# Two of the four weight sums of a block chunk made by accumulating transfers, and 23 block chunks in place of 20

## The chip, the cores and the metric

The kernel runs on one core of one Trainium2 chip. The metric is the device time of one execution in microseconds (us), lower is better. Engines are named as the profile names them: PE is TensorE's matmuls and PEld its weight loads, DVE is VectorE, ACT is ScalarE, POOL is GpSimd and SP is SyncE; the last two issue transfers (DMAs) here. PSUM is the memory that TensorE writes to, in eight banks of 512 fp32 values per partition.

## The reference

One layer over 512 tokens of 1024 channels, with 256 context tokens that give further keys and values. One combined projection yields ten parts of 1024 columns; half of them feed a gated convolution, the others a neighbourhood attention and the gates that merge both.

```python
h = _rmsnorm(x, pre_g[i]) * (1.0 + sc[:, None, :]) + sh[:, None, :]
...
parts = _split_in(h @ w_in[i])           # b, c, x, z_a | q, k, v, z_b | g_a, g_b
q = _apply_rope(_heads(parts[4]), cos, sin)
k = _apply_rope(_heads(parts[5]), cos, sin)
...
attn = _neighbourhood_attention(q, k, v, k_c, v_c, rpb[i])
y_a = (jax.nn.silu(z_a) * b_gate * _dwconv3(c_gate * x_in, conv_w, conv_b)) @ w_out_conv
y_b = (jax.nn.silu(z_b) * attn_o) @ w_out_attn
merged = jax.nn.sigmoid(g_a) * y_a + jax.nn.sigmoid(g_b) * y_b
x = x + gt[:, None, :] * _rmsnorm(merged @ w_o, post_g[i])
```

## The kernel before

**Products.** Every fp32 operand is split into a high part (a ScalarE cast to a type that TensorE multiplies at full speed, L67) and a low part (a VectorE subtraction, L68). A product is three matmuls: high by high, high by low, low by high.

**Chunks.** The weights of the projections come as 45 chunks of 1024 rows by 256 columns, that is two units of 128 output channels. Each is loaded as two `raw` tiles of 512 KB, for the upper and the lower 512 rows (`Chunk`, L87; three buffers of `raw`, four of the split weights `w`). They are named by what they yield: `cx` and `bz` for the convolution (two of its parts each), `qk` (a query and a key unit), `v`, `zb` (the attention's gate), `g0` to `g7` (the merge gates), `y0` to `y7` (both out projections). The last stage, after the y chunks, is the out projection with `w_o`.

- A plain chunk takes 2 x 8 x 3 = 48 matmuls of 512 columns.
- A block chunk halves rows, tokens and units, so that the weights are four blocks: B11 and B12 (columns 0 to 127 and 128 to 255 of the upper raw tile; `b11`, `b12` in the code), B21 and B22 (of the lower one). Seven block products in place of eight are made of four blocks or sums on the weights' side and as many on the tokens' side: T1 = B11 + B12, T2 = T1 + B22, T3 = B12 + B22, T4 = B21 + T2. Each of the seven is 12 matmuls of 256 columns, 84 in all (`product`, L287). The sums of the tokens are made once (`block_sums`), those of the weights for every chunk, in place in the raw tiles, on VectorE: L100 (T1), L103 (T2), L107 (T3), L108 (T4).

`pair` (L291) is the block chunk's program. It multiplies B11, B21, T1 and T2 in its first half, copies two banks into SBUF as snapshots on the way (L298, L301, L303, on ScalarE), then T4, T3 and B22 in its second half, with a copy (L309) and VectorE's combining operations (L312, L315). It uses three banks `a`, `b`, `e`. `Chunk.first` prepares what the first half needs and runs one chunk ahead; `Chunk.second` splits T3, T4 and B22 when the pair begins. A `qk` chunk is the exception: its B12 is kept for the context keys, so T3's sum is made in `second`. The chunk after it is loaded by `chunk.more()` in the middle of the pair. `paired` (L231) says which chunks are blocks: all g, qk3, qk4 and qk6, zb0 to zb2, cx and bz from 5, 20 in all.

**Stages.** At the start, conditioning and norms beside the first conv chunks, in an order written by hand. Then the attention: 64 steps of (pair of heads p, head, 128 queries), eight to each p, with the chunks of `plan` (L217) spread over the steps of their p; scores, softmax, transposes and the gather of values stand between them. `later` holds back queries and keys by some steps, until their rope is done. Behind the last step comes zb3, then g2 and g3, beside which the slices of the conv result `u` and of the attention are split into `us0` to `us7` and `as0` to `as7`; then y0, g4, y1, g5, ... in the order of `merge` (L236).

**Order.** Apart from the start, a scheduler places the instructions on each engine; the program's text gives their priority. Each engine then runs its own list in that order, and an instruction that waits holds up what stands behind it. SP's queue carries the weight loads. GpSimd's queue carries rope's accumulating transfers (L624, `tc<-tb`) and the copies of queries and keys between partitions, some 104 transfers in all.

Of the kernel before, what the change touches and what calls it, by code (L numbers as in the profile page):

```python
# [12 lines left out]
ALU = mybir.AluOpType  # L13
AX = mybir.AxisListType

P = 128
D = 1024
KT = 8
S = 512
# [8 lines left out]
def layer(ctx: ExitStack, tc, xp, ctxt, ctxT, cc, wmod, small, wfirst, win, wout, wo, rel, tab, out):  # L28
    nc = tc.nc
# [33 lines left out]

    def split(H, L, src, scale=None):

        if scale is None:
            nc.scalar.copy(H, src)  # L67
            nc.vector.tensor_sub(L, src, H.bitcast(F32))  # L68
        else:
            nc.scalar.mul(H, src, scale)  # L70
            nc.vector.scalar_tensor_tensor(
                out=L, in0=src, scalar=scale, in1=H.bitcast(F32), op0=ALU.mult, op1=ALU.subtract
            )
# [7 lines left out]
    class Chunk:  # L81
# [14 lines left out]
        def first(self, keep=False):  # L96
            (b11, b12), (b21, b22) = self.b = [(r[:, :, :P], r[:, :, P:]) for r in self.raws]
            t, sums = (wtile([P, 2, 2, 4, P]) for _ in range(2))
            split(t[:, 0, 0], t[:, 0, 1], b11)
            nc.vector.tensor_add(b11, b11, b12)  # L100
            split(sums[:, 0, 0], sums[:, 0, 1], b11)
            split(t[:, 1, 0], t[:, 1, 1], b21)
            nc.vector.tensor_add(b11, b11, b22)  # L103
            split(sums[:, 1, 0], sums[:, 1, 1], b11)
            self.keep = keep
            if not keep:
                nc.vector.tensor_add(b12, b12, b22)  # L107
            nc.vector.tensor_add(b21, b21, b11)  # L108
            self.B = {"B11": t[:, 0], "B21": t[:, 1], "T1": sums[:, 0], "T2": sums[:, 1]}
            return self  # L110

        def second(self):
            t, last = (wtile([P, 2, 2, 4, P]) for _ in range(2))
            (_, b12), (b21, b22) = self.b
            if self.keep:
                split(last[:, 1, 0], last[:, 1, 1], b12)
                nc.vector.tensor_add(b12, b12, b22)
            for n, x, b in (("T3", t[:, 0], b12), ("T4", t[:, 1], b21), ("B22", last[:, 0], b22)):
                split(x[:, 0], x[:, 1], b)
                self.B[n] = x  # L120
            self.B["B12"] = last[:, 1]

# [108 lines left out]
    def paired(n, i):  # L231
        return n == "g" or n == "qk" and i in (3, 4, 6) or n == "zb" and i < 3 or n in ("cx", "bz") and i > 4

# [48 lines left out]
    blocks_h = {}  # L282
# [8 lines left out]

    def pair(c1, c2, w=None):

        w = w or chunk().B
        a, b, e = (pj()[:, :256] for _ in range(3))
# [7 lines left out]
        nc.scalar.copy(c2[:, first], a)  # L303
        nc.vector.tensor_add(c1[:, first], c1[:, first], b)
        chunk.more()
        yield
        product(b, A22, w["T4"], True)
        product(a, blocks_h["S3"], w["T3"], False)
        nc.scalar.copy(c1[:, second], a)  # L309
        product(e, blocks_h["S4"], w["B22"], False)  # L310
        for cols, x in ((second, c1[:, second]), (first, e)):
            nc.vector.scalar_tensor_tensor(  # L312
                out=c2[:, cols], in0=c2[:, cols], scalar=-1.0, in1=x, op0=ALU.mult, op1=ALU.subtract
            )
        nc.vector.tensor_add(c1[:, second], c1[:, second], b)  # L315

# [339 lines left out]
    def keys_queries(p):  # L656
# [3 lines left out]
        if blocks:  # L660
            for _ in pair(q, k, w.B):
                yield
# [19 lines left out]

        def keys(src, cols):
            split(ks[0][:, cols], lows[:, cols], src)

        def rest():
            keys(k, slice(0, S))
            nc.gpsimd.dma_start(ks[1][lo], ks[0][hi])
# [513 lines left out]
```

## Time and profile before

| | |
|---|---|
| median of 3 runs | 709.33 us (709.26 to 709.7) |
| the profiled execution | 710.12 us |
| its span, first to last instruction | 708.3 us |
| granted TensorE clock, mean | 0.999 |
| DVE, second busiest engine | 585.2 us, 83% |
| ACT | 437.2 us, 62% |
| block products (L287) on PE | 216 us in 1680 matmuls |
| T3 and T4 sums (L107, L108) on DVE | 25.3 us in 37 additions |

The profile is of one execution. Its page gives the busy time of each engine, the chain of work that ended last (followed back from the last instruction to what released each step), and the costliest groups of instructions: the line, the engine, the operation with its output and input by the program's names, how many, the busy time and the mean, the idle time before them and what ended it. The trace can be asked for the same in any stretch, for what one tile waits for, and for the instructions in order of time.

### The profile page before, as it was taken

How to read it: one execution, taken by the hardware profiler on the slowest of the kernel's cores; microseconds unless marked ns; L12 is line 12 of the kernel's file. 1: busy time of each engine (PE TensorE's matmuls, PEld its weight loads, DVE VectorE, ACT ScalarE, POOL GpSimd, SP SyncE). 2: the span in 40 equal slices, each digit the busy share in tenths (PEclk: the TensorE clock that was granted, in tenths of full speed). 3: DMA queues.
4: the chain of work that ended last, by engine and by line, in shares of the span. 5: the costliest groups of instructions: out<-in, count | busy, mean ns of one | idle time of the engine just before them, and what ended most of it. 6: DMA issues, size and time to landing. Idle time of an engine off the chain costs nothing.

```text
span 708.3 us, 11424 instructions
## 1 busy us (share of the span) xinstructions
PE 695.4 (98%) x4196; PEld 618.5 (87%) x4196; DVE 585.2 (83%) x1114; ACT 437.2 (62%) x868; POOL 66.9 (9%) x110
## 2 busy tenths in 40 slices
PE   7999999999999999999999999999999999999996
PEld 4888888888889989898999999999898899988885
DVE  6979997668599989978898797999799675665996
ACT  6566632656577678765886676888694444442563
POOL 0000002240130310401302103000000000000000
PEclk9999999999999999999999999999999999999999
DMA  8996896565341563642636436313733233570013
GB/s 341 407 348 228 281 339 172 134 163 143 100 99 29 137 157 119 151 125 61 168 106 171 94 127 154 104 60 98 250 115 120 88 119 120 186 261 30 31 59 120
DMA packets 37466, 108.27 MB, mean 153 GB/s; under 512 B 5025, under 2 KB 5281, under 8 KB 37410
## 3 DMA queue, kind: packets, MB, share of 16 engines
q1 hardware_dynamic: 28946, 92.20, 38.0%
q0 software_dynamic: 8320, 15.21, 10.7%
q8 instruction: 33, 0.54, 0.3%
q14 instruction: 23, 0.19, 0.1%
q10 hardware_dynamic: 144, 0.13, 0.1%
HBM read 87.07 MB, written 5.24 MB: 130 GB/s over the span
## 4 chain that ended last, share of the span: by engine, by line
PE 88%; DVE 5%; DMA 3%; ACT 2%; issue 1%; SPq 0%; POOL 0%; DVEq 0%; ACTq 0%
PE ps L287 23%; PE ps L162 11%; PE ps L163 11%; PE ps L164 11%; PE ps L175 6%; PE ps L1006 5%; PE ps L771 4%; PE ps L180 3%; PE ps L752 3%; PE ps L715 3%; PE ps L194 2%; PE ps L422 2%; PE ps L426 2%; PE ps L423 2%; DMA fraw<-in_wfirst 1%; DVE w L68 1%
## 5 line engine op out<-in xcount | busy, mean ns | idle before, releaser
L67 ACT CAST w<-raw 128x512 fp32r<-128x512 f32 (+1 forms) x193 | 137.2, 731 | 91.4 <-PE ps L164 30.7
L68 DVE TENSOR_TENSOR w<-raw,w 128x512 fp32r<-128x512 f32 (+1 forms) x193 | 156.3, 824 | 41.8 <-ACT w L67 41.0
L287 PE MATMUL ps<-S,w 128*128 128x256 f32 x960 | 122.0, 283 | 1.2 <-ACT tc L303 1.2
L287 PEld LDWEIGHTS ps<-S,w 128*128 128x128 f32 x960 | 118.1, 192 | 1.5 <-ACT tc L303 1.4
L287 PE MATMUL ps<-h,w 128*128 128x256 f32 x720 | 94.2, 284 | 0.5 <-DVE tc L315 0.4
L287 PEld LDWEIGHTS ps<-h,w 128*128 128x128 f32 x720 | 89.9, 191 | 2.5 <-DVE tc L315 0.9
L162 PE MATMUL ps<-h,w 128*128 128x512 f32 x208 | 81.5, 392 | 0.0
L164 PE MATMUL ps<-h,w 128*128 128x512 f32 x208 | 81.2, 390 | 0.0
L163 PE MATMUL ps<-h,w 128*128 128x512 f32 x208 | 81.0, 390 | 0.0
L624 POOL DMA_DIRECT2D tc<-tb x32 | 28.8, 1175 | 301.9 <-DVE tc L622 182.6
L164 PEld LDWEIGHTS ps<-h,w 128*128 128x128 f32 x208 | 39.0, 188 | 8.2
L67 ACT CAST TH<-ps 128x512 fp32r<-128x512 f32 x64 | 36.0, 588 | 16.5 <-PE ps L752 16.4
L162 PEld LDWEIGHTS ps<-h,w 128*128 128x128 f32 x208 | 39.1, 188 | 8.0
L163 PEld LDWEIGHTS ps<-h,w 128*128 128x128 f32 x208 | 39.1, 188 | 7.9
L731 DVE CUSTOM_DVE_ANT_1 ps<-ps,bt 128x512 f32<-128x512 f32 x56 | 38.8, 694 | 8.4 <-PE ps L715 8.2
L745 ACT ACTIVATE pt<-pt,z 128x512 f32<-128x512 f32 x64 | 42.9, 721 | 4.6 <-DVE z L743 4.3
L68 DVE TENSOR_TENSOR TL<-ps,TH 128x512 fp32r<-128x512 f32 x64 | 42.4, 681 | 0.8 <-ACT TH L67 0.7
L752 PE MATMUL ps<-ident,pt 128*128 128x128 f32 x256 | 33.2, 273 | 0.0
L175 PE MATMUL ps<-w,h 128*128 128x512 f32 x128 | 32.3, 394 | 0.0
L752 PEld LDWEIGHTS ps<-ident,pt 128*128 128x128 f32 x256 | 29.3, 140 | 2.1
L738 ACT ACTIVATE pt<-ps,m 128x512 f32<-128x512 f32 x32 | 22.0, 689 | 10.8 <-DVE m L731 10.0
L771 PE MATMUL ps<-TH,V 128*128 128x256 f32 (+1 forms) x96 | 28.4, 318 | 0.0
(249 smaller groups left out, 1387.6 us busy)
## 6 DMA issues: line engine op xcount, KB each, us to landing
raw<-in_win SPq DMA_DIRECT2D x74, 512.0 KB, 4.5
wm<-in_wmod SPq DMA_DIRECT2D x34, 512.0 KB, 6.4
raw<-in_wout SPq DMA_DIRECT2D x16, 512.0 KB, 3.8
bt<-in_rel SPq DMA_DIRECT2D x16, 256.0 KB, 3.0
tc<-tb POOLq DMA_DIRECT2D x32, 128.0 KB, 3.8
B<-in_wo SPq DMA_DIRECT2D x8, 512.0 KB, 7.4
fraw<-in_wfirst SPq DMA_DIRECT2D x8, 384.0 KB, 8.7
qd<-qd POOLq DMA_DIRECT2D x24, 128.0 KB, 2.4
```

Source lines behind the costliest of these rows:

```text
L67: nc.scalar.copy(H, src)
L68: nc.vector.tensor_sub(L, src, H.bitcast(F32))
L162: nc.tensor.matmul(ps, lhsT=H[k][:, cs], rhs=mH[k], start=k == 0, stop=False)
L163: nc.tensor.matmul(ps, lhsT=H[k][:, cs], rhs=mL[k], start=False, stop=False)
L164: nc.tensor.matmul(ps, lhsT=L[k][:, cs], rhs=mH[k], start=False, stop=k == KT - 1)
L175: nc.tensor.matmul(ps, lhsT=mH[k][:, ts], rhs=both[k].rearrange("p a c -> p (a c)"), start=k == 0, stop=False, skip_group_check=True,)
L287: nc.tensor.matmul(ps, lhsT=w[:, x, k], rhs=act[y][k], start=start and k + o == 0, stop=k == 3 and o == 2, skip_group_check=True,)
L731: nc.vector.tensor_tensor_reduce(out=s3, in0=s3, in1=bt[:, e::4 - e][:, 0:2], scale=-1.0, scalar=3.0e38, op0=ALU.add, op1=ALU.min, accum_o ...
L745: nc.scalar.mul(x, x, z[:, i:i + 1])
L752: nc.tensor.transpose(tp[:, c], pt[:, c * P:(c + 1) * P], ident)
L771: nc.tensor.matmul(o3[:, dst], lhsT=V[p][:, kt, h], rhs=src(t), start=n == 0 and t is TH, stop=n == len(work) - 1 and t is TL,)
L1006: nc.tensor.matmul(out, lhsT=a(x, k, ts), rhs=w[y][k // 2][:, k % 2, cols], start=start and k + o == 0, stop=k == 3 and o == 2, skip_group ...
```

## The change

**Transfers for two sums.** T3 and T4 are no longer added on VectorE. `nc.gpsimd.dma_start(b12, b22, accum_op=ALU.add)` adds B22 to B12 inside SBUF, and the same adds T2 to B21. The first is issued behind T1's sum, the second behind T2's sum, both on GpSimd's queue, 256 KB each. T3 of a `qk` chunk stays on VectorE, since its B12 is needed. So that a block is one run of values in each partition, the host lays out the block chunks' weights by blocks.

**Later casts.** `second` splits B22 alone (and B12 of a `qk` chunk). The splits of T3 and T4 go to a new `third`, called behind the first half's snapshots, and their casts are pinned there with `tc.keep_in_program_order`: the scheduler can't move them ahead of the snapshots or behind what follows in the text. In the second half the products are now B22, T3, T4 in place of T4, T3, B22.

**More blocks.** qk5, qk7 and zb3 become block chunks, 23 in all.

**Keys.** The cast of a block chunk's keys (in `rest`) is pinned in the text's order too.

```diff
--- before.py
+++ after.py
@@ -61,10 +61,12 @@
     usc = [dr.tile([P, S], F32, name=f"usc{j}") for j in range(KT)]
     asc = [dr.tile([P, 2, S], F32, name=f"asc{g}") for g in range(2)]
 
-    def split(H, L, src, scale=None):
+    def split(H, L, src, scale=None, pinned=False):
 
         if scale is None:
-            nc.scalar.copy(H, src)
+            cast = nc.scalar.copy(H, src)
+            if pinned:
+                tc.keep_in_program_order(cast)
             nc.vector.tensor_sub(L, src, H.bitcast(F32))
         else:
             nc.scalar.mul(H, src, scale)
@@ -94,31 +96,38 @@
             return tuple([t[i // 4][:, i % 4, y] for i in k] for y in range(2)) + ([t[i // 4][:, i % 4] for i in k],)
 
         def first(self, keep=False):
-            (b11, b12), (b21, b22) = self.b = [(r[:, :, :P], r[:, :, P:]) for r in self.raws]
+            (b11, b12), (b21, b22) = self.b = [
+                [x[:, 2 * u:2 * u + 2].rearrange("p k (x c) -> p (k x) c", c=P) for u in range(2)] for x in self.raws
+            ]
             t, sums = (wtile([P, 2, 2, 4, P]) for _ in range(2))
             split(t[:, 0, 0], t[:, 0, 1], b11)
             nc.vector.tensor_add(b11, b11, b12)
+            if not keep:
+                nc.gpsimd.dma_start(b12, b22, accum_op=ALU.add)
             split(sums[:, 0, 0], sums[:, 0, 1], b11)
             split(t[:, 1, 0], t[:, 1, 1], b21)
             nc.vector.tensor_add(b11, b11, b22)
+            nc.gpsimd.dma_start(b21, b11, accum_op=ALU.add)
             split(sums[:, 1, 0], sums[:, 1, 1], b11)
             self.keep = keep
-            if not keep:
-                nc.vector.tensor_add(b12, b12, b22)
-            nc.vector.tensor_add(b21, b21, b11)
             self.B = {"B11": t[:, 0], "B21": t[:, 1], "T1": sums[:, 0], "T2": sums[:, 1]}
             return self
 
         def second(self):
-            t, last = (wtile([P, 2, 2, 4, P]) for _ in range(2))
-            (_, b12), (b21, b22) = self.b
+            last = wtile([P, 2, 2, 4, P])
+            (_, b12), (_, b22) = self.b
             if self.keep:
                 split(last[:, 1, 0], last[:, 1, 1], b12)
                 nc.vector.tensor_add(b12, b12, b22)
-            for n, x, b in (("T3", t[:, 0], b12), ("T4", t[:, 1], b21), ("B22", last[:, 0], b22)):
-                split(x[:, 0], x[:, 1], b)
+            split(last[:, 0, 0], last[:, 0, 1], b22)
+            self.B["B22"], self.B["B12"] = last[:, 0], last[:, 1]
+
+        def third(self):
+            t = wtile([P, 2, 2, 4, P])
+            (_, b12), (b21, _) = self.b
+            for n, x, b in (("T3", t[:, 0], b12), ("T4", t[:, 1], b21)):
+                split(x[:, 0], x[:, 1], b, pinned=True)
                 self.B[n] = x
-            self.B["B12"] = last[:, 1]
 
 
     behind = None
@@ -229,7 +238,7 @@
         "cx": lambda j: win[2 * j], "bz": lambda j: win[2 * j + 1],
     }
     def paired(n, i):
-        return n == "g" or n == "qk" and i in (3, 4, 6) or n == "zb" and i < 3 or n in ("cx", "bz") and i > 4
+        return n == "g" or n == "qk" and i > 2 or n == "zb" or n in ("cx", "bz") and i > 4
 
     order = [(win[i], False) for i in range(8)] + [(qk(0), False), (vz(0, 0), False)]
     order += [(where[n](i), n if paired(n, i) else False) for f in plan for n, i in f] + [(vz(3, 1), paired("zb", 3))]
@@ -289,9 +298,10 @@
                     skip_group_check=True,
                 )
 
-    def pair(c1, c2, w=None):
-
-        w = w or chunk().B
+    def pair(c1, c2, c=None):
+
+        c = c or chunk()
+        w = c.B
         a, b, e = (pj()[:, :256] for _ in range(3))
         first, second = slice(0, 256), slice(256, S)
         product(a, A11, w["B11"], True)
@@ -302,16 +312,17 @@
         product(a, blocks_h["S2"], w["T2"], False)
         nc.scalar.copy(c2[:, first], a)
         nc.vector.tensor_add(c1[:, first], c1[:, first], b)
+        c.third()
         chunk.more()
         yield
-        product(b, A22, w["T4"], True)
+        product(e, blocks_h["S4"], w["B22"], False)
         product(a, blocks_h["S3"], w["T3"], False)
         nc.scalar.copy(c1[:, second], a)
-        product(e, blocks_h["S4"], w["B22"], False)
-        for cols, x in ((second, c1[:, second]), (first, e)):
+        for cols, x in ((first, e), (second, c1[:, second])):
             nc.vector.scalar_tensor_tensor(
                 out=c2[:, cols], in0=c2[:, cols], scalar=-1.0, in1=x, op0=ALU.mult, op1=ALU.subtract
             )
+        product(b, A22, w["T4"], True)
         nc.vector.tensor_add(c1[:, second], c1[:, second], b)
 
     def both_units():
@@ -658,7 +669,7 @@
         q, k = both_units()
         blocks = paired("qk", p)
         if blocks:
-            for _ in pair(q, k, w.B):
+            for _ in pair(q, k, w):
                 yield
             rope(q, q)
             rope(k, k)
@@ -680,11 +691,11 @@
                     nc.gpsimd.dma_start(t[1][o], t[0][hi])
                 nc.gpsimd.dma_start(t[0][hi], t[0][lo])
 
-        def keys(src, cols):
-            split(ks[0][:, cols], lows[:, cols], src)
+        def keys(src, cols, pinned=False):
+            split(ks[0][:, cols], lows[:, cols], src, pinned=pinned)
 
         def rest():
-            keys(k, slice(0, S))
+            keys(k, slice(0, S), blocks)
             nc.gpsimd.dma_start(ks[1][lo], ks[0][hi])
             nc.gpsimd.dma_start(ks[1][hi], lows[hi])
             nc.gpsimd.dma_start(ks[0][hi], lows[lo])
@@ -1143,6 +1154,9 @@
     ui = units(a["w_in"][0]).copy()
     ui[q:v] = ui[q:v][..., channels]
     win = chunks(ui, order)
+
+    for n in [*range(10, 16), *(16 + 4 * (p // 2) + p % 2 for p in range(3, 8)), *range(19, 32, 4), *range(32, 40)]:
+        win[n] = win[n].reshape(128, 2, 4, 2, 128).transpose(0, 1, 3, 2, 4).reshape(128, 8, 256)
     uo = np.concatenate([units(a["w_out_conv"][0]), units(a["w_out_attn"][0])])
 
     wfirst = np.ascontiguousarray(win[:3].transpose(2, 1, 0, 3)).reshape(8, 128, 768)
```

The scheduler's lists move in the tail. The next rows are ScalarE's list around g2 and g3 before: `raw_5753` and `raw_5754` are g2's two raw tiles, `raw_5938` is g3's first, `us` are the slices of `u`, `ur` their sources, and L782 is zb3's tanh.

```order
L67 CAST w_5875<-raw_5753 128x512
L67 CAST w_5875<-raw_5754 128x512
L67 CAST us1_5959<-ur1_5851 128x512
L67 CAST us2_5962<-ur2_5852 128x512
L67 CAST us3_5965<-ur3_5853 128x512
L782 ACTIVATE tb_5842<-ps_5817 128x512
L67 CAST w_5876<-raw_5754 128x512
L67 CAST us4_6009<-ur4_5854 128x512
L298 COPY g2_5874<-ps_5883 128x256
L67 CAST us5_6012<-ur5_5855 128x512
L67 CAST us6_6015<-ur6_5856 128x512
L67 CAST w_5942<-raw_5938 128x512
```

After the change the list has these rows from the third snapshot of g2 on (L313); `raw_5952` and `raw_5953` are g2's tiles, `raw_6127` is g3's first, and `as` are the slices of the attention.

```order
L313 COPY g2_6063<-ps_6067 128x256
L67 CAST w_6122<-raw_5952 128x512
L67 CAST w_6122<-raw_5953 128x512
L67 CAST us7_6207<-ur7_6046 128x512
L67 CAST as0_6284<-ta_6047 128x512
L67 CAST as1_6287<-tb_6048 128x512
L67 CAST as2_6290<-ta_6049 128x512
L320 COPY g2_6063<-ps_6067 128x256
L67 CAST as3_6293<-tb_6050 128x512
L67 CAST w_6131<-raw_6127 128x512
L67 CAST as4_6337<-at4_3893 128x512
L67 CAST as5_6340<-at4_3893 128x512
```

g2's casts of T3 and T4 (`w_6122`) stood ahead of the pair's first snapshot and stand behind its third now; g3's first cast (B11) stood behind us6 and stands behind us7 and as0 to as3.

ScalarE's list in zb3 after the change, where zb3 is a block chunk: `raw_5788` and `raw_5789` are its tiles, `tc` its two units, and `raw_5952` and `w_5956`, `w_5957` belong to g2.

```order
L308 COPY tc_5887<-ps_5892 128x256
L67 CAST w_5819<-raw_5788 128x512
L311 COPY tc_5888<-ps_5894 128x256
L313 COPY tc_5888<-ps_5892 128x256
L67 CAST w_5947<-raw_5788 128x512
L67 CAST w_5947<-raw_5789 128x512
L67 CAST w_5956<-raw_5952 128x512
L787 COPY ta_5983<-ps_5970 64x512
L67 CAST us0_6145<-ur0_6039 128x512
```

Two new casts, T3 from `raw_5788` and T4 from `raw_5789`, stand between zb3's last snapshot and g2's B11; before, zb3 was plain and its casts were done ahead of its matmuls.

TensorE's list in y3 changes at the fourth slice of `u`: `w_6862` and `w_6863` are y3's two halves, `ps_6927` is the unit fed by `u` and `ps_6953` the one fed by the attention.

```order
L171 MATMUL ps_6927<-us4_6198,w_6863 128x512
L172 MATMUL ps_6927<-us4_6198,w_6863 128x512
L171 MATMUL ps_6953<-as0_6284,w_6862 128x512
L172 MATMUL ps_6953<-as0_6284,w_6862 128x512
L173 MATMUL ps_6953<-as0_6284,w_6862 128x512
L173 MATMUL ps_6927<-us4_6198,w_6863 128x512
```

Before, the three of us4 stood together; now the matmul with the low part of y3's second half (L173) has three of the other unit ahead of it.

## The prediction

> **What bounds the kernel now.** I read the page's head first, then the chain, then the busy time by stretches.
>
> ```profile
> span 708.3 us, 11424 instructions
> ...
> PE 695.4 (98%) x4196; PEld 618.5 (87%) x4196; DVE 585.2 (83%) x1114; ACT 437.2 (62%) x868; POOL 66.9 (9%) x110
> ...
> PE 88%; DVE 5%; DMA 3%; ACT 2%; issue 1%; SPq 0%; POOL 0%; DVEq 0%; ACTq 0%
> ```
>
> TensorE is busy for 98% of the span and the chain is 88% TensorE: VectorE's sums, which the change takes away, are not what ends last. So the change can gain in two ways only: fewer matmul microseconds, and fewer waits of TensorE. It loses wherever TensorE must wait for a weight block that comes later than now. The stretches show how much room there is.
>
> ```profile
> core 0: us, PE busy (x) PEld busy (x) DVE busy (x) ACT busy (x) POOL busy (x), PEclk, DMA share, GB/s
> ...
> 321.00:366.20 45.20, 45.20 (x315) 41.99 (x313) 40.18 (x84) 32.25 (x68) 8.32 (x13) 1.00 0.44 121
> ...
> 502.00:515.20 13.20, 13.20 (x65) 11.12 (x65) 12.08 (x22) 8.53 (x16) 0.00 (x0) 1.00 0.73 247
> 515.20:535.50 20.30, 20.30 (x170) 20.30 (x169) 19.41 (x33) 16.67 (x33) 0.00 (x0) 1.00 0.45 141
> 535.50:546.40 10.90, 10.90 (x50) 9.01 (x50) 10.46 (x25) 4.59 (x7) 0.00 (x0) 1.00 0.16 53
> 546.40:556.50 10.10, 10.10 (x85) 10.08 (x85) 5.80 (x9) 5.15 (x9) 0.00 (x0) 1.00 0.55 174
> ```
>
> 321 to 366 holds qk5, zb1 and cx6; 502 to 515 is the plain chunk zb3; 515 to 535 are the pairs g2 and g3; then come the plain y0 and the pair g4. VectorE is 89% busy in the first, and 92% and 96% in the next two: from 502 to 535 it works 31.5 us of 33.5 and is nearly the bound.
>
> **Three more block chunks.** y0 takes 10.9 us as a plain chunk, g4 10.1 as a block: 0.8 saved for each of qk5, qk7 and zb3, **-2.5 us** (48 matmuls of 512 columns against 84 of 256, so no more than a pitch can change). VectorE and ScalarE pay for it; see below.
>
> **The keys' casts.** TensorE's largest wait in the middle of the span stands in these rows of the timeline.
>
> ```profile
> 249.75 0.62 ACT L67 CAST ks<-tc 128x512 fp32r<-128x512 f32 x1 [3.87 <-DMA tc<-tb]
> ...
> 250.54 0.38 ACT L303 COPY tc<-ps 128x256 f32<-128x256 f32 x1
> ...
> 250.97 3.13 PE L287 MATMUL ps<-S,w 128*128 128x256 f32 x24 [1.21 <-ACT tc L303]
> ...
> 258.45 1.22 PE L287 MATMUL ps<-h,w 128*128 128x256 f32 x8 [0.43 <-DVE tc L315]
> ```
>
> ScalarE stood 3.87 us at a keys' cast whose rope transfer had not landed, the snapshot behind it (L303) came late, and TensorE waited 1.21. Pinned, that cast stands behind zb0's gate: **-1.2 us**, at most 1.64 with the row below it, whose bank wait I leave as it is.
>
> **The sums taken from VectorE.**
>
> ```profile
> L108 DVE TENSOR_TENSOR raw<-raw 128x512 f32<-128x512 f32 x20 | 13.7, 686 | 0.2
> ...
> L107 DVE TENSOR_TENSOR raw<-raw 128x512 f32<-128x512 f32 x17 | 11.6, 684 | 1.1 <-DMA raw<-in_win 1.1
> ```
>
> 37 sums, 25.3 us of VectorE, go to the transfers. Beside a TensorE that is never without work this is worth nothing by itself; it pays for the new blocks: each adds 5 to 6 subtractions, 2 sums and 4 half-width operations. In 321 to 366 that is about +6 for qk5 and -3 for five sums, 43 of 44.4 us. Sums and subtractions are hidden under TensorE as long as VectorE keeps ahead; without that cover each costs its 0.6.
>
> **What the sums cost as transfers.** The trace has no accumulation of 256 KB; the nearest are rope's of 128 KB, in the stretch 240 to 520.
>
> ```profile
> L624 POOL DMA_DIRECT2D tc<-tb x20: 885/1194/1860, 241.1 to 432.7; - x20
> ...
> DMA to landing us min/median/max: 2.6/3.4/6.9
> ```
>
> Half the size lands in 2.6 to 6.9, so 256 KB lies between 2.6 and 13.8 (twice the slowest). I take 5, the median and half as much again. 41 of them go through GpSimd's queue, ahead of keys' transfers; GpSimd is 9% busy and those have some 9 us to spare, so the queue itself costs nothing; if it does, scores wait. What is exposed is the cast of T4: it is pinned right behind the first snapshots, and while it waits for b21 everything behind it on ScalarE waits too.
>
> The Trainium skill (page "DMA: Bandwidth & Descriptors", section "Anatomy of one DMA") gives a transfer that GpSimd issues about 2.0 us plus its bytes at 436 GB/s, by estimate 2.6 for 256 KB. The trace disagrees already at half the size, median 3.4. By the page's price neither wait for T4 in the tail below would be left, and the sum would be 2.6 us lower.
>
> **Tiles that are held longer.** Each chunk's two raw tiles come from three buffers, so a chunk's second tile lands where the chunk before had its first (b11, b12).
>
> ```profile
> SPq L87 <- DVE w L68: 258.6, 68, 14.3
> ...
> raw<-in_win SPq DMA_DIRECT2D x74, 512.0 KB, 4.5
> ...
> raw<-in_wout SPq DMA_DIRECT2D x16, 512.0 KB, 3.8
> ```
>
> The loads wait for nothing but that cast (68 times, for L68). Now it is T3's cast before the pair begins; after the change it stands behind the first snapshots. The rows of g4, next, give the steps.
>
> ```profile
> 545.39 0.33 SPq L87 DMA_DIRECT2D raw<-in_wout  x1
> 546.22 3.04 PE L287 MATMUL ps<-h,w 128*128 128x256 f32 x24
> ...
> 549.33 1.05 ACT L67 CAST w<-raw 128x1024 fp32r<-128x1024 f32 x1 [0.45 <-PE ps L287]
> ...
> 550.41 1.23 DVE L68 TENSOR_TENSOR w<-raw,w 128x1024 fp32r<-128x1024 f32 x1 [0.63 <-ACT w L67]
> ...
> 552.17 0.37 ACT L303 COPY g<-ps 128x256 f32<-128x256 f32 x1 [1.07 <-PE ps L287]
> ...
> 557.37 1.06 ACT L809 ACTIVATE g<-g 128x1024 f32<-128x1024 f32 x1 [0.91 <-DVE g L312]
> ```
>
> The load issued at 545.39, ahead of the pair. After: snapshot 5.95 us into the pair (552.17 less 546.22), +0.37, T3's cast 0.6, its subtraction 0.7: the load goes out at 7.6 instead of -0.8. For y1 to y4 it lands 3.8 later, at 11.4; ScalarE first does the tanh of g4 (ends about 11.8: pair's end 10.1, last sum 0.4, tanh 1.06), then cast 1.05 and subtraction 1.23, to 14.1. TensorE needs that low part at 10.1 + 12 x 0.227 + 0.45 = 13.3: 0.8 late, of which three matmuls of the second unit, put there by the new order, fill 0.7. I take 0.2 for each of y0 to y4, **+1.0** (0 to 4).
>
> In the attention phase a pair follows the last by 13 us or more; there the second tile lands at 7.6 + 4.5 = 12.1 and is cast in time. What is left are waits like the 0.43 above, for the bank that the last sum (L326) frees, which VectorE now does behind the next chunk's T2 sum: **+1.0** over some 15 pairs (-0.5 to +4).
>
> **The tail, zb3 to g3.** Here three pairs follow each other, and the slices of `u` and attention that y0 needs (16 casts, 16 subtractions) lie between.
>
> ```profile
> 489.94 3.04 PE L287 MATMUL ps<-h,w 128*128 128x256 f32 x24
> ...
> 496.97 1.67 PE L287 MATMUL ps<-h,w 128*128 128x256 f32 x12
> ...
> 518.75 0.38 SPq L87 DMA_DIRECT2D raw<-in_win  x1
> ...
> 523.79 0.62 ACT L67 CAST w<-raw 128x512 fp32r<-128x512 f32 x1 [0.75 <-DMA raw<-in_win]
> ...
> 525.12 1.66 ACT L67 CAST w<-raw 128x512 fp32r<-128x512 f32 x3
> ...
> 527.80 1.89 DVE L68 TENSOR_TENSOR w<-raw,w 128x512 fp32r<-128x512 f32 x3
> ```
>
> Casts in a row come every 0.55, subtractions every 0.6 us (1.66 and 1.89 for three). From g1's start (489.94), with the orders shown with the change and nothing late, zb3 would start at 12.3, g2 at 24.3 (a gather of 1.9 lies within zb3) and g3 end at 44.4. Step by step: g1's T3 is done at 7.8, zb3's second tile lands at 12.4 and its T2 sum ends at 16.4, three operations behind it; the transfer into b21 lands at 21.4. zb3's snapshots end at 19.6, T3's cast at 20.2, T4's waits until 21.4, and g2's and the `us` casts stand behind. g2's second tile, free at 20.9, lands at 25.4; its B21 is ready at about 27.6 where TensorE stands at 26.6; with the sequel g2 ends at 36.2, **1.8 late**. In g3 B11's cast stands behind us7 and as0 to as3 and its low part is there at 37.9 (1.7 late); B21 and T2 cost 0.9 more; T2's sum ends at 42.1, b21 lands at 47.1, and T4's cast ends at 47.7 where TensorE comes at 46.3 (1.4): **4.0 late**. Together **+5.8**. It can't be under 1.65: even with idle engines g3's B21 has its low part at 7.6 + 4.5 + 0.6 + 0.7 = 13.4 from g2's start, and TensorE wants it at 11.75 (the pair's 10.1, g3's first twelve matmuls 1.52, one with the high part 0.13). It can reach 9, if the transfers take 7.
>
> **Sum.** -2.5 - 1.2 + 1.0 + 1.0 + 5.8 = +4.1. The profiled execution took 710.12 us, 1.8 of it around its span of 708.3, and stands 0.8 above the median of 709.33, to which I add: **713.4 us**.
>
> **Rivals.** (1) *The tail absorbs it, faster.* VectorE has 25 us less to do, and keeps so far ahead that only the 1.65 of pure latency is left, with 0.3 for the y chunks and none in the attention phase: -2.5 - 1.6 + 1.95 = -2.15, 707.2, down to 705 if the order fills even that. For it: 1.5 us of VectorE's 33.5 were idle before and the new blocks cost about what the sums save. Against it: VectorE's idling comes from waiting in order, which no saved sum removes. It decides at a tail under 2.3. Chance 0.24. (2) *The transfers land as fast as the fastest row*, 2.6: no wait for T4 in zb3 (1.2) nor in g3 (1.4), tail 3.2, y 0.5, attention 0: 709.3, no change. That is also what the skill's price would give, nearly. Chance 0.16. (3) *My forecast*, 711 to 716: 0.42. (4) *ScalarE is blocked in every pair.* If b21 lands 7 us or more after the T2 sum, T4's pinned cast holds back the exponentials and casts of the attention phase as the keys' cast did above; there 3.9 us of blocking cost TensorE 1.2, so 1.2 less half for ten pairs is +6 more, 719 or so. Chance 0.18. That the freed VectorE alone gains nothing is in all four.
>
> **Numbers.** 0.2% (1.4 us) is about what a measurement of this kernel tells from no change. Faster by more: (1), 0.24. Within: (2), 0.16. Slower: (3) and (4), 0.60. The range leaves out the lower end of (1) and the far end of (4): 705.5 to 719.5.
>
> **What would show it.** Right: gaps of TensorE between g2 and y0 that end with casts of `w` or with VectorE's subtraction of `w`, loads of the second tiles issued some 7.6 us into a pair, ScalarE waiting for a transfer `raw<-raw`, and no wait for `ks<-tc` over 1 us. Wrong: TensorE without gaps from 515 to 560, or the largest gaps in the attention phase; transfers `raw<-raw` that land in under 3 us, or over 7.

## The result, and the profile after

The changed kernel is slower: 726.76 us median of 5 runs (725.0 to 729.31) against 709.55 (709.26 to 710.0), ratio 1.0245, 95% interval [1.0231, 1.0259]. That is +17.2 us, where +4.1 was forecast. Its profiled execution took 726.44 us.

These are lines of the page of the changed kernel: its head, the shares of the chain that ended last, the casts of weights with ScalarE's idle time before them, and the transfers that add.

```profile
span 724.7 us, 11820 instructions
...
PE 703.7 (97%) x4304; PEld 625.4 (86%) x4304; DVE 579.0 (80%) x1114; ACT 446.9 (62%) x897; POOL 103.1 (14%) x151
...
PE 73%; DVE 11%; DMA 9%; ACT 5%; issue 2%; POOL 0%; DVEq 0%; ACTq 0%
...
L67 ACT CAST w<-raw 128x512 fp32r<-128x512 f32 (+1 forms) x210 | 144.6, 712 | 77.8 <-DMA raw<-in_win 20.8
...
raw<-raw POOLq DMA_DIRECT2D x41, 256.0 KB, 3.3
```

TensorE was 88% of the chain and is 73%; VectorE, DMA and ScalarE have grown from 10% to 25%: the span grew by waits. TensorE's busy time grew too, from 695.4 to 703.7 us, part of it at half its clock (below). A transfer lands in 3.3 us as a rule, less than the 5 that I took.

Where the time goes is best seen by stages. The table is worked out from the records of TensorE, in us: *attention* is from the first transposes of the 64 steps to those of the last; *zb3* from there to g2's first matmul; *g2* to g3's first; *g3* its first to its last; *y* from there to the end of y7. Each row is one profiled execution, and the ratio is that of the runs. Single executions of the changed kernel lie up to 4.3 us apart, those of the kernel before up to 1.8 over all runs, so a microsecond between two rows of the attention stage tells little; g3 and y agree to the tenth wherever nothing is late in them.

| kernel | ratio to before [95%] | attention | zb3 | g2 | g3 | y |
|---|---|---|---|---|---|---|
| before | 1 | 351.5 | 13.8 | 10.1 | 10.2 | 128.4 |
| **changed** | 1.0245 [1.0231, 1.0259] | 355.4 | 13.5 | 16.5 | 13.0 | 132.1 |
| sums on VectorE, e1 | 1.0299 [1.0275, 1.0324] | 362.8 | 14.0 | 11.0 | 15.6 | 131.8 |
| no pins, e2 | 1.0088 [1.0073, 1.0104] | 354.3 | 12.8 | 13.6 | 10.2 | 128.4 |
| early casts, e3 | 1.0114 [1.0097, 1.0131] | 355.2 | 12.8 | 16.8 | 10.2 | 128.4 |
| reload by GpSimd, e4 | 1.0220 [1.0201, 1.0239] | 357.3 | 13.3 | 17.0 | 11.0 | 132.3 |
| before + keys pinned, e5 | 0.9995 [0.9986, 1.0003] | 350.8 | 13.7 | 10.1 | 10.2 | 128.4 |
| before + 3 blocks, e6 | 1.0055 [1.0042, 1.0067] | 353.5 | 12.9 | 11.0 | 11.1 | 128.0 |
| e2 + g2 on VectorE, e8 | 1.0051 [1.0037, 1.0064] | 354.2 | 12.8 | 10.3 | 11.8 | 128.4 |
| before + transfers, e9 | 1.0055 [1.0040, 1.0071] | 353.6 | 13.7 | 10.1 | 12.0 | 128.4 |
| T4 alone late, e10 | 1.0281 [1.0264, 1.0298] | 365.3 | 13.2 | 16.7 | 10.7 | 128.4 |
| T3 alone late, e11 | 1.0095 [1.0080, 1.0110] | 350.6 | 13.1 | 17.6 | 10.2 | 129.5 |
| changed, g2 on VectorE, e13 | 1.0188 [1.0162, 1.0213] | 355.0 | 13.6 | 11.0 | 14.8 | 132.1 |
| put together, e14 | 1.0027 [1.0017, 1.0037] | 350.2 | 13.1 | 10.5 | 12.8 | 128.0 |

The changed kernel loses 3.9 us in the attention stage (it should have gained 1.6 from qk5 and qk7), 6.4 in g2, 2.8 in g3 and 3.7 behind g3.

g2 first. The timeline of the changed kernel, one row for each run of like instructions: start, duration, engine, line, and in brackets the idle time before with what ended it. From TensorE, ScalarE, GpSimd and SP:

```profile
528.45 0.50 PE L296 MATMUL ps<-S,w 128*128 128x256 f32 x2 [1.93 <-ACT w L67]
530.26 0.80 PE L296 MATMUL ps<-h,w 128*128 128x256 f32 x2 [1.31 <-ACT w L67]
...
527.78 0.62 ACT L67 CAST w<-raw 128x512 fp32r<-128x512 f32 x1 [2.29 <-DMA raw<-raw]
529.59 0.62 ACT L67 CAST w<-raw 128x512 fp32r<-128x512 f32 x1 [1.20 <-DMA raw<-raw]
...
518.83 0.89 POOL L106 DMA_DIRECT2D raw<-raw  x1 [7.27 <-DVE us L70]
521.21 0.87 POOL L110 DMA_DIRECT2D raw<-raw  x1 [1.50 <-DVE tc L326]
...
514.78 0.33 SPq L89 DMA_DIRECT2D raw<-in_win  x1
515.16 3.29 SPq L898 DMA_DIRECT2D ur<-usc  x7
```

Read from below: SP sends g2's second weight tile at 514.78, when zb3's late cast of T3 has freed a buffer, and seven of the eight reloads of `u` right behind it. Into these GpSimd issues g2's two adding transfers. In the kernel before, the whole reload had gone out ahead of all this:

```profile
500.60 4.60 SPq L887 DMA_DIRECT2D ur<-usc  x8
```

The late cast is not the whole of that shift: in e6, with early casts and zb3 as a block, the reload starts at 509.0. Asked for g2's two transfers alone, the trace of the changed kernel gives (columns: durations of the issue; then the landing as min/median/max)

```profile
L106 POOL DMA_DIRECT2D raw<-raw x1: 886/886/886, 518.8 to 518.8; - x1
DMA to landing us min/median/max: 8.9/8.9/8.9
...
L110 POOL DMA_DIRECT2D raw<-raw x1: 872/872/872, 521.2 to 521.2; - x1
DMA to landing us min/median/max: 8.4/8.4/8.4
```

8.9 and 8.4 in place of 3.3. ScalarE stands at the two casts and TensorE behind them, 3.2 us. And from 528.9 to 535.7 TensorE runs at half its clock (the column ahead of the DMA share in the stretches of 1 us):

```profile
528.00:529.00 1.00, 0.50 (x2) 0.30 (x2) 0.57 (x1) 0.40 (x1) 0.00 (x0) 0.94 1.10 412
529.00:530.00 1.00, 0.00 (x0) 0.00 (x0) 0.12 (x1) 0.41 (x1) 0.00 (x0) 0.50 1.00 406
...
534.00:535.00 1.00, 1.00 (x7) 1.00 (x6) 0.66 (x2) 1.00 (x3) 0.00 (x0) 0.50 0.29 119
535.00:536.00 1.00, 0.75 (x4) 0.46 (x3) 0.64 (x2) 1.00 (x3) 0.00 (x0) 0.64 0.00 0
536.00:537.00 1.00, 0.56 (x4) 0.56 (x5) 1.00 (x3) 1.00 (x2) 0.00 (x0) 1.00 0.00 0
```

From 528.45 to g3's first matmul at 535.12, g2's last 24 matmuls take 5.4 us beside the wait, where 24 of 0.12 are 2.9. Waits and clock are 5.7 of g2's 6.4 us.

The y chunks: rows of the changed kernel in g4, which begins at 560.63, from ScalarE and SP, and of TensorE in y0.

```profile
566.58 0.37 ACT L313 COPY g<-ps 128x256 f32<-128x256 f32 x1 [1.07 <-PE ps L296]
566.85 2.09 ACT L67 CAST w<-raw 128x512 fp32r<-128x512 f32 x3
...
568.22 0.33 SPq L89 DMA_DIRECT2D raw<-in_wout  x1
...
551.76 0.50 PE L171 MATMUL ps<-us,w 128*128 128x512 f32 x1 [0.84 <-ACT w L67]
553.02 0.50 PE L173 MATMUL ps<-us,w 128*128 128x512 f32 x1 [0.29 <-DVE w L70]
```

y1's second tile goes out 7.6 us into the pair (568.22 less 560.63), to the tenth as forecast. y0's went out later still, at 545.46, 10.3 us into g3, which itself had waits; TensorE waits 0.84 and 0.29 for it.

The keys: ScalarE and TensorE of the changed kernel, where before the keys' cast stood for 3.87 us.

```profile
248.00 0.72 ACT L72 ACTIVATE qd<-tc 128x448 fp32r<-128x448 f32 x2 [2.55 <-DMA tc<-tb]
249.46 0.37 ACT L311 COPY tc<-ps 128x256 f32<-128x256 f32 x1 [0.73 <-DVE qe L73]
...
249.88 1.33 PE L296 MATMUL ps<-S,w 128*128 128x256 f32 x9 [1.38 <-ACT tc L311]
```

The keys' cast has gone from there, and the scaling of the queries, which waits for the same rope, stands there now. TensorE waits 1.38 where it waited 1.21.

### The profile page after: what moved, and what is told of

It is laid out like the page before. It is cut to its first block, busy times and chain, and to the rows that moved or that the text cites. A ratio compares the mean times of both kernels' runs of the same rounds, so it can differ in the third digit from the quotient of the medians.

```text
span 724.7 us, 11820 instructions
## 1 busy us (share of the span) xinstructions
PE 703.7 (97%) x4304; PEld 625.4 (86%) x4304; DVE 579.0 (80%) x1114; ACT 446.9 (62%) x897; POOL 103.1 (14%) x151
## 4 chain that ended last, share of the span: by engine, by line
PE 73%; DVE 11%; DMA 9%; ACT 5%; issue 2%; POOL 0%; DVEq 0%; ACTq 0%
PE ps L296 16%; PE ps L173 9%; PE ps L171 9%; PE ps L172 9%; PE ps L184 6%; PE ps L1017 5%; DMA raw<-in_win 5%; DVE w L70 4%; PE ps L189 3%; ACT w L67 3%; PE ps L782 2%; PE ps L763 2%; PE ps L726 2%; PE ps L433 2%; PE ps L437 2%
## 5 line engine op out<-in xcount | busy, mean ns | idle before, releaser
L70 DVE TENSOR_TENSOR w<-raw,w 128x512 fp32r<-128x512 f32 (+1 forms) x210 | 164.1, 799 | 59.2 <-ACT w L67 58.3
L67 ACT CAST w<-raw 128x512 fp32r<-128x512 f32 (+1 forms) x210 | 144.6, 712 | 77.8 <-DMA raw<-in_win 20.8
L296 PE MATMUL ps<-S,w 128*128 128x256 f32 x1104 | 144.6, 286 | 5.5 <-ACT w L67 2.4
L296 PEld LDWEIGHTS ps<-S,w 128*128 128x128 f32 x1104 | 137.6, 192 | 9.0 <-ACT w L67 3.0
L296 PE MATMUL ps<-h,w 128*128 128x256 f32 x828 | 112.1, 287 | 4.2 <-ACT w L67 1.3
L296 PEld LDWEIGHTS ps<-h,w 128*128 128x128 f32 x828 | 105.1, 193 | 7.2 <-DVE w L70 2.1
L171 PE MATMUL ps<-h,w 128*128 128x512 f32 x160 | 62.5, 391 | 0.0
L173 PE MATMUL ps<-h,w 128*128 128x512 f32 x160 | 62.5, 390 | 0.0
L172 PE MATMUL ps<-h,w 128*128 128x512 f32 x160 | 62.3, 390 | 0.0
L106 POOL DMA_DIRECT2D raw<-raw x18 | 15.9, 885 | 182.3 <-DVE w L70 91.5
L173 PEld LDWEIGHTS ps<-h,w 128*128 128x128 f32 x160 | 30.0, 188 | 6.3
L171 PEld LDWEIGHTS ps<-h,w 128*128 128x128 f32 x160 | 30.0, 188 | 6.2
L172 PEld LDWEIGHTS ps<-h,w 128*128 128x128 f32 x160 | 30.0, 188 | 6.2
L110 POOL DMA_DIRECT2D raw<-raw x23 | 20.4, 889 | 80.0 <-DVE w L70 20.6
L749 ACT ACTIVATE pt<-ps,m 128x512 f32<-128x512 f32 x32 | 22.1, 690 | 15.0 <-DVE m L742 14.8
## 6 DMA issues: line engine op xcount, KB each, us to landing
tc<-tb POOLq DMA_DIRECT2D x32, 128.0 KB, 3.7
```

Source lines behind the costliest of these rows:

```text
L67: cast = nc.scalar.copy(H, src)
L171: nc.tensor.matmul(ps, lhsT=H[k][:, cs], rhs=mH[k], start=k == 0, stop=False)
L172: nc.tensor.matmul(ps, lhsT=H[k][:, cs], rhs=mL[k], start=False, stop=False)
L173: nc.tensor.matmul(ps, lhsT=L[k][:, cs], rhs=mH[k], start=False, stop=k == KT - 1)
L296: nc.tensor.matmul(ps, lhsT=w[:, x, k], rhs=act[y][k], start=start and k + o == 0, stop=k == 3 and o == 2, skip_group_check=True,)
```

## The experiments

The text on the change said of the pin that the scheduler can't put the cast behind what follows. That is too strong: `keep_in_program_order` sets one edge, from the ScalarE instruction ahead of it in the text. T3's cast thus stays behind the third snapshot, and T4's behind T3's; both can go later.

**The transfers or the late casts?** e1 puts both sums back on VectorE where the transfers were issued.

```diff
-                nc.gpsimd.dma_start(b12, b22, accum_op=ALU.add)
+                nc.vector.tensor_add(b12, b12, b22)
...
-            nc.gpsimd.dma_start(b21, b11, accum_op=ALU.add)
+            nc.vector.tensor_add(b21, b21, b11)
```

> Both sums go back to VectorE at the very places where the transfers are issued; late pinned casts, 23 block chunks and pinned keys stay. Theory A (the transfers are the price: T3 and T4 arrive late and ScalarE stands at their pinned casts): g2's two waits for the casts (1.93 and 1.31 us) and the half clock behind them go, and the y chunks' too: 714 to 717. Theory B (the price is the late place of the casts, which holds the second raw tile until 7.6 us into a pair and with it SP's queue, so the reloads of u and attention start at 515 and not at 501): g2 no longer collides, worth some 6 us, but the second tiles stay late: 719 to 721, with VectorE's 25 us more on top. Rival C (the three more block chunks are the price): 725 or more.

731.41 us: slower than the changed kernel, against A and B; only rival C allowed such a number. g2 lost its stall (11.0), but the attention stage grew by 7.4 and g3 by 2.6. With 23 blocks and late casts the transfers are worth some 4 us (0.54% by the ratios); they aren't the price of the change as a whole. Nor are the blocks by themselves (e6, below). The y stage is at 131.8 as with transfers, so its 3.7 us have nothing to do with them.

**The pins.** e2 unpins the two casts.

```diff
-                split(x[:, 0], x[:, 1], b, pinned=True)
+                split(x[:, 0], x[:, 1], b)
```

> The casts of T3 and T4 aren't pinned; their place in the text, the transfers and all else stay. Theory A: the scheduler can put other ScalarE work ahead of them, but TensorE needs them as late: 722 to 726. Theory B: the place in the text still lies behind the snapshots, so the tiles are held as long: within 2 us of the changed kernel, 725 to 728. If the pin by itself were the price: under 718.

715.68 us: 11 less. Neither A nor B had it, and the third expectation did, that the pin by itself is the price. B was wrong on what holds an unpinned cast: the place in the text alone doesn't, and the scheduler moved casts ahead of the snapshots again (in g2 both). g3 and y are at the old 10.2 and 128.4. g2 still takes 13.6: the reload starts at 509.4, and g2's two transfers land in 7.5 and 7.2 us.

**The old order**, with the transfers kept: e3 splits T3 and T4 in `second`, unpinned, and multiplies T4, T3, B22 in the second half.

```diff
-            split(last[:, 0, 0], last[:, 0, 1], b22)
+            for n, x, b in (("T3", t[:, 0], b12), ("T4", t[:, 1], b21), ("B22", last[:, 0], b22)):
+                split(x[:, 0], x[:, 1], b)
+                self.B[n] = x
...
-        c.third()
```

> The casts of T3 and T4 go back to the start of the pair, unpinned, and the second half is multiplied in the old order T4, T3, B22; the transfers, 23 block chunks and pinned keys stay. Theory A: T4 is now needed 2.9 us earlier than in the changed kernel and its transfer takes 3.3 us as before: no better, 724 or more. Theory B: the second raw tiles are free before the pair, SP's queue and the reloads move back to 501, the tail's 9.7 us of waits and the y chunks' 3 go: 710 to 714.

717.81 us, between the two: g3 and y are free of waits, as B said, but g2 takes 16.8 and the attention stage 355.2. In g2 the reason is not that T4 is wanted sooner. The casts stand ahead of the first snapshot (L303) again and wait there for transfers that land in 7.1 and 7.2 us beside the reload (from 509.5), and TensorE waits for that snapshot:

```profile
520.09 0.62 ACT L67 CAST w<-raw 128x512 fp32r<-128x512 f32 x1 [3.38 <-DMA raw<-raw]
522.48 1.14 ACT L67 CAST w<-raw 128x512 fp32r<-128x512 f32 x2 [1.77 <-DMA raw<-raw]
...
525.61 0.35 ACT L303 COPY g<-ps 128x256 f32<-128x256 f32 x1
```

TensorE's wait is 3.96 us. The pins, which cost so much elsewhere, keep this wait out of the first half of a pair.

**The reload.** e4 sends the reloads of `u` by GpSimd's queue.

```diff
-        nc.sync.dma_start(reloaded[k], usc[k])
+        nc.gpsimd.dma_start(reloaded[k], usc[k])
```

> The eight reloads of u go through GpSimd's queue in place of SP's, so they no longer stand behind the held weight load; all else as in the changed kernel. Theory B: they start near 502, g2's two transfers land in 3.3 us in place of 8.4 to 8.9, the 3.2 us of waits for the casts and the half clock behind them (529 to 535) go: 719 to 722. Theory A (transfers late whatever else runs): 725 to 728.

724.77 us, a miss for B's number. The first reload went out at 513.07 and not at 502, behind zb3's second transfer on the same queue, and three of the eight came between and behind g2's two. Those still landed in 4.7 and 5.5 us, and g2 took 17.0: this time ScalarE stood 2.12 us at a cast of `u` for one of the last reloads, with the third snapshot and T3's cast behind it, and TensorE waited 3.05. The run moved the collision and did not remove it.

**The parts one by one**, on the kernel before: the keys' pin (e5), the three blocks (e6: `paired` as in the change), the transfers with the blocks' layout (e9: the two additions as `dma_start`, nothing else).

> The kernel before with the casts of block chunks' keys pinned, and nothing else. As predicted blind: the wait of 3.87 us at the keys' cast goes and TensorE's 1.2 behind it, 708.1 to 708.5. Rival, after the trace of the changed kernel (ScalarE stood 2.55 us at the same place at the queries' scaling, which waits for the same rope): the wait changes its owner, 709 to 710.

> The kernel before with qk5, qk7 and zb3 as block chunks; sums on VectorE, casts, order and layout of before. If the blocks are sound by themselves: 709.5 less 2.5, some 707. If the blocks are part of the price because VectorE, 89 to 96% busy there, has no room for their sums and subtractions: 711 to 716, with TensorE's waits at zb3 and g2 and in the steps of qk5 and qk7.

> The kernel before with nothing but the two sums as transfers and the blocks' layout: 20 block chunks, old order of casts and products, keys not pinned. If a transfer is as good as VectorE's sum as long as the casts are early: 709 to 711. If its 3.3 us are late for the casts, which the scheduler places for a shorter transfer, ScalarE stands in line before them at many pairs: 713 to 717.

e5 took 708.87 us, no change that these runs can tell. e6 took 713.2 and e9 713.26, each 3.9 us slower by its ratio. They add up: 3.9 + 3.9 - 0.4 = 7.4, and e3, which holds these three, lost 8.1. In e6 zb3 as a block does save: it takes 12.9 in place of 13.8. The waits behind them take more. TensorE and ScalarE of e6 in the step of qk7:

```profile
443.11 1.10 PE L287 MATMUL ps<-S,w 128*128 128x256 f32 x7 [1.46 <-ACT tc L303]
...
441.89 0.62 ACT L67 CAST ks<-tc 128x512 fp32r<-128x512 f32 x1 [3.33 <-DMA tc<-tb]
```

The keys' cast that the pin was put on stands for its rope here too. For e9, ScalarE's idle time before the casts of line 67 by what ended it (us, times) has an entry that before has none of:

```profile
  DMA raw<-in_win: 20.7, 17
  DMA raw<-raw: 16.8, 13
```

In e9 zb3 is a plain chunk and the reload goes out at 500.9. g2's transfers land beside it in 6.4 and 4.6 us, but at 512.4 and 513.7, ahead of g2's start at 517.1, and g2 takes 10.1. In these runs, then, g2's stall comes only with both, transfers for its sums and a reload that comes late. With the transfers alone (e9) it is not there; with a late reload alone (e1, e6, e8, e13, e14) g2 takes 10.3 to 11.0; with both (changed, e2, e3, e10, e11, and e4 in its own way) 13.6 to 17.6.

**g2's two transfers.** e8 is e2 with g2's sums alone on VectorE, e13 the changed kernel with the same (chunk 34 of the list is g2).

```diff
+            if add:
+                nc.vector.tensor_add(b12, b12, b22)
-            if not keep:
+            elif not keep:
...
+        self.ahead[n] = c.first(kind == "qk", n == 34) if kind else c.split()
```

> The changed kernel with the casts of T3 and T4 unpinned (as in the run e2_unpinned, 715.7) and g2's two sums alone on VectorE; all other sums stay transfers. If g2's stall there (TensorE waits 1.72 us and then runs at half its clock for some us, 3.5 in all) comes from g2's two transfers that share the DMA engines with the reload of u and land in 7.2 to 7.5 us: the stall goes, 712 to 713. If it comes from anything else that is late in g2: 715 to 716.

> The changed kernel, both pins kept, with g2's two sums alone on VectorE. g2 took 16.66 us in place of 10.24 there: if its two transfers of 8.9 and 8.4 us beside the reload are the cause, some 6 us go and it ends at 720 to 722. Under theory H the second tiles of g2 and g3 stay late, so only the part that ScalarE stood at the casts goes: 722 to 725.

e8: 712.6 us, and g2 falls from 13.6 to 10.3, while g3 goes from 10.2 to 11.8. e13: 722.36, g2 falls from 16.5 to 11.0, while g3 goes from 13.0 to 14.8: part of it comes back a pair later, as the second expectation had it. In e13 ScalarE waits there for g3's own second tile, which had gone out 8.4 us into g2 and took 6.0:

```profile
532.99 0.50 PE L301 MATMUL ps<-h,w 128*128 128x256 f32 x2 [1.88 <-ACT w L67]
...
532.32 1.14 ACT L67 CAST w<-raw 128x512 fp32r<-128x512 f32 x2 [1.77 <-DMA raw<-in_win]
```

**One late cast at a time.** e11 pins T3 alone, e10 T4 alone (T4 put first in the loop, so that its edge reaches the snapshot).

```diff
-            for n, x, b in (("T3", t[:, 0], b12), ("T4", t[:, 1], b21)):
-                split(x[:, 0], x[:, 1], b, pinned=True)
+            for n, x, b in (("T4", t[:, 1], b21), ("T3", t[:, 0], b12)):
+                split(x[:, 0], x[:, 1], b, pinned=n == "T4")
```

> The changed kernel with T4's cast alone kept behind the first half's snapshots; T3's cast is free to go ahead of them, so the buffer of the first raw tile, in which the next chunk's second tile lands, comes free before the pair. Theory H (the price of the pins is the held buffer): loads issued ahead of the pairs again, no waits at the y chunks, 715 to 718 like the run without pins. Theory L (the price is ScalarE standing at T4's pinned cast until the transfer has landed): 723 to 727 like the changed kernel.

> The mirror image: T3's cast alone is kept behind the snapshots and holds the first raw tile's buffer; T4's cast is free. Theory H: second tiles issued some 7.6 us into a pair, waits at the y chunks and at g3 as in the changed kernel, 722 to 727. Theory L: 715 to 718.

The totals look like theory L: 729.09 with T4 late, 715.55 with T3 late. But the stages say something else. Behind g3 *both* are free of most of the changed kernel's 3.7 us (0 and 1.1 are left), so there it takes both casts late: with one of them early, one buffer comes free early, and the next chunk's second tile uses it. y1's goes out 2.3 us into g4 in e10, 5.1 in e11 (right behind T4's subtraction) and 7.6 in the changed kernel, and the losses behind g3 follow: 0, 1.1, 3.7. All of e10's loss against e11 lies in the attention stage, 14.7 us. e10 there, from ScalarE, VectorE and TensorE:

```profile
256.86 1.14 ACT L67 CAST w<-raw 128x512 fp32r<-128x512 f32 x2 [3.77 <-DMA raw<-raw]
...
258.03 0.69 DVE L70 TENSOR_TENSOR w<-raw,w 128x512 fp32r<-128x512 f32 x1 [3.38 <-ACT w L67]
258.64 0.41 DVE L326 TENSOR_TENSOR tc<-tc,ps 128x256 f32<-128x256 f32 x1
...
259.11 1.23 PE L296 MATMUL ps<-h,w 128*128 128x256 f32 x4 [2.76 <-DVE tc L326]
```

ScalarE stands at a cast for a transfer, VectorE at that cast's subtraction, and behind the subtraction stands the sum (L326) that frees the bank for TensorE. e10 has five such waits in that stage, of 0.9 to 2.8 us, and behind three of them TensorE runs at half its clock for 3.4 us. ScalarE's idle time at transfers is nearly the same in e11 (16.7 us, 12 times) as in e10 (15.6 us, 7 times): what it costs depends on what stands behind it. In g2 both runs are no better than the changed kernel (16.7 and 17.6): the cast that is free stands ahead of a snapshot and waits there for a transfer that took 7.7 to 8.0 us beside the reload.

**Put together**, e14: transfers up to zb3 with T3 alone pinned, as in e11; from g2 on sums on VectorE and no pins.

> Put together from the runs: 23 block chunks, keys pinned; up to zb3 the sums by transfer with T3's cast alone kept behind the snapshots (in the run e11_pin_t3 TensorE stood 2.0 us ahead of the kernel before where g2 begins); from g2 on both sums on VectorE and no pins. If the tail's price is g2's transfers beside the reload (6.4 us of the changed kernel) and the held raw tiles (6.5 us in g3 and the y chunks), both are gone and the tail costs what it did with the blocks alone (1.4 us): 708 to 709.5, level with the kernel before. If VectorE has no room for the sums in g2 and g3 beside the slices of u and attention: 711 to 714.

711.12 us: g2 and y came out as hoped, and the attention stage is 1.3 us below before. That qk5 and qk7 pay there is not shown by this: the profiled execution of e14 lies 0.9 us under its median and that of before 0.8 over its own, and e5, without the new blocks, took 350.8. But g3 took 12.8 (0.7 of it three matmuls of y0 that were put into it, as in e6). In g3 two waits, 0.8 and 0.4 us, end with a snapshot that stood behind g2's tanh and with a subtraction that stood behind three of `u`, which is the second expectation. e14 is the best with 23 blocks, and still 0.27% slower than the kernel before.

## Why the prediction was wrong

The direction was right and the size wrong by a factor of four; the time lies outside the range. Of the signs set out beforehand, those of being right all appeared, and one of being wrong: transfers `raw<-raw` that land in over 7 us, the two of g2. Step by step:

- **The tail, zb3 to g3: +5.8 forecast, 9.7 measured** (8.9 more than before in the table, and 0.8 saved by zb3 as a block). The failed step is that of g2, "1.8 late", where 6.4 were lost. I had the late second tile and T4's blocked cast, but put the block into zb3 and g3, with a transfer of 5 us everywhere. I did not count what else SP's queue carries behind the held tile: the reload, issued from 500.6 to 505.2 before (all of it ahead of g2's sums), moves to 515 and runs into the two transfers, which land in 8.9 and 8.4 us. Some 8 us of that move come with zb3 as a block (e6), the rest with its late casts. e8 and e13 show that it takes the two transfers (without them g2 is at 10.3 and 11.0), and e9 speaks for the late reload (there it is early, but zb3 and the order of the casts differ as well). My range for a transfer, 2.6 to 13.8, held both values; one value for all places was the mistake. And the half clock, 2.5 us, was in no term. g3, 4.0 forecast, came out at 2.8. The 4.0 has a slip in it: by the prediction's own times TensorE, late by 1.7 and 0.9, comes to T4 at 36.2 + 2.6 + 8.6 (72 matmuls of 0.12) = 47.4 and not at 46.3, so T4's cast at 47.7 costs 0.3 and not 1.4. The tail would then be +4.7 and the sum +3.0, farther from the result.
- **The y chunks: +1.0 forecast (0 to 4), 3.7 measured.** The mechanism was right: the tile that goes out 7.6 us into the pair. y1, y3 and y4 lost 0.2 each, as taken. y0 lost 1.7, its tile being later still, and y2 0.6, and the pairs g4 to g7 0.2 each, which I had at nothing.
- **The attention phase: +1.0 forecast, about 5.5 measured** (3.9 more than before and 1.6 that the two new blocks save; the keys' -1.2 is a point of its own, next). The waits that I named are there (for the bank behind L326: 0.68 and 0.78 us), and so are others: 0.75 and 1.04 at the first snapshots behind qk5 and qk7. The waits of over 0.1 us sum to 4.9 us in this stage, against 1.6 before; the rest of the 5.5 stands in no wait that the profile shows. Parts of it are the price of the blocks (e6: 3.6, counted the same way) and of the transfers (e9: 2.2). How they share out with the pins depends on the order that the scheduler makes, 350.6 to 365.3 us among kernels that differ in a pin; it can't be told from these runs what the next order would give.
- **The keys' casts: -1.2 forecast, nothing.** I took the wait for the keys' own. It belongs to the rope transfer, and the next instruction that needs it, the queries' scaling, stood in its place. I did not ask which instruction in ScalarE's line would wait for it next.
- **The blocks: -2.5 forecast.** zb3 falls by 0.9 in e6, as forecast for each; for qk5 and qk7 no run shows the saving by itself. "VectorE and ScalarE pay for it" was priced at nothing in qk5 and qk7; alone, the three blocks cost 3.9 us net.
- **The sums as transfers** were to cost nothing but T4's cast. Alone they cost 3.9 us (e9), though most land sooner than I took (median 3.3). Beside 23 blocks and late casts they are worth 4 (e1).
- **Rival (4)**, ScalarE blocked in every pair, named the right kind of wait, but not in the changed kernel, where ScalarE stood for a `raw<-raw` transfer 3.5 us in all, both times in g2. It is what e3, e9, e10 and e11 do, where casts are free to be early.

What the pins do is now clear in the tail: e2 against the changed kernel, 11 us, of which 3.7 behind g3, 2.8 in g3, 2.9 in g2, 0.7 in zb3 and 1.1 in the attention stage (the last within what single executions differ by). Behind g3 the held buffers are shown as the cause, by the load times of e10, e11 and the changed kernel, which the losses follow. In g3 they are shown in e13 by the late load; in the changed kernel it rests on the same reading of the timeline.

## What to carry to other kernels

A late cast is also a late buffer, and so is a plain chunk that becomes a block. On an in-order queue all that stands behind the load which waits for that buffer is late with it: list that queue's other transfers and ask what they will run into. When a wait is taken from one instruction, find the event that it waited for and the next one in line that needs it. A transfer has no one duration: price it at each place by what else is in flight there.

## What the runs showed of the hardware

TensorE's granted clock can fall to half after a wait of under 2 us within otherwise steady work. Waits of 1.38 (changed kernel, 248), 1.46 (e6, 441), 1.58 (e10, 503), 1.68 (e2, 456) and 1.88 us (e4, 444) left it at 1.00; waits of 1.72 (e2, 521), 1.75 and 2.07 (e1, 540 and 249) and 1.88 us (e13, 531) were followed by 3.4 us at 0.50. The records of the clock in the traces tell these apart. All its changes in a run lie at whole multiples of 3.41 us from one another. Cut into such windows, each wait that put 1.72 us or more of idling into one window was followed by the half clock from that window's end on, twelve times in these runs; none that put 1.68 or less into a window at full clock was. e4's wait of 1.88 us was split by a window's end into 1.35 and 0.53. The half clock then lasted one window, or two (6.8 us) where the next held more idling, 0.8 to 1.5 us, as in g2 of the changed kernel. By estimate a fall of one window costs half of it, 1.7 us, beside the wait. The Trainium skill, page "TensorE: Matmul & The Clock Gate", section "Part 1: The HAM clock gate (the "warmup" mystery)", has the gate close after an idle window of some 3.4 us that runs freely. The 3.41 us agree with the length of that window, and the two waits of 1.88 us with its running freely; that 1.72 us of idling, half a window, was enough to close the gate does not agree.

An adding transfer of 256 KB within SBUF landed in 3.3 us (median of the 41 of the changed kernel, the fastest in 3.2). The two that were issued behind seven loads of 256 KB took 8.9 and 8.4, and in four other runs the two beside the reload took 7.1 to 8.0 (e2, e3, e10, e11).
